# Gate/up products: high and low activations side by side in one 512-wide matmul

## The chip, the cores and the metric

One core of a Trainium2 chip runs the whole kernel in one launch. The metric is device time in microseconds. The kernel before took 2802.89 us, the median of 3 runs (2801.14 to 2803.51).

## The reference, cut to what matters

The program is one layer of a hybrid encoder on 512 tokens of width 2048: an adaLN-conditioned token mixer, a layer norm, then a SwiGLU sublayer of width 5632, all in float32. The change lies in the first half of the SwiGLU:

```python
def swiglu(h, w_gate, w_up, w_down):
    return (jax.nn.silu(h @ w_gate) * (h @ w_up)) @ w_down
...
x = layer_norm(ALPHA * x + (1.0 + gt_m) * y, ln1_g[l], ln1_b[l])
h = x * (1.0 + sc_f) + sh_f
y = swiglu(h, w_gate[l], w_up[l], w_down[l])
```

## The kernel before, in words

**Precision.** Every float32 operand is cut into a rounded high part (ScalarE, a copy to the matmul's type) and the remainder as low part (VectorE, a subtraction): `split`, lines 275 to 277. A product is then three matmuls in `mm3` (lines 239 to 243): high x high, and the two cross terms. For gate/up the weights are stationary (128x128) and the activations are moving.

**Seven products.** Gate and up each multiply 2048 x 512 activations (transposed: `m_hi`, `m_lo`) by 2048 x 5632 weights. This is done as a 2x2 block scheme with seven products in place of eight: weight blocks 11, 12, 21, 22 and their sums S1 to S4, against quarters of the activations and their block sums R4, R6, R7 (R5 goes into the m tiles). A quarter has 256 tokens, so each moving operand is 256 columns wide. The order in a group is `SEVEN = ("p1", "q7", "r6", "p2", "q5", "q4", "p3")` (line 127). p1, p2, q5 and p3 read the m tiles, q7, r6 and q4 the block sums, whose tiles hold high and low side by side. V (p1, r6, q5, p3), Y (q7, q4) and A (p2) are three PSUM banks per group (`CHAIN`); V is read between its products.

**Groups and order.** There are 44 groups `("gu", n)`: n // 2 is the pair of column blocks, n % 2 is gate or up. A gate and the up behind it make a pair: the up's results are multiplied into the gate's Silu. The first four groups (`NPRE`) run in another order, beside the end of the first layer norm; the other 40 run their seven products one behind the other. All is written out by hand and each engine works in program order. The main loop (lines 1601 to 1638) does for each product `step`:

- `prepare(step + 3)`: the high part (ScalarE, `whi`) and low part (VectorE, `wlo`) of the weights three products ahead, 4 buffer pairs in turn;
- `gu_product`: 8 k-steps of `mm3`, 24 matmuls;
- `gu_use`: what follows the product: ScalarE copies or Silu, VectorE adds, subtractions and multiplies, straight from PSUM;
- `add_behind`: VectorE sums of weight blocks: S3 and S1 three steps ahead of a group, S2 two ahead, S4 two steps into it (1024 wide, lines 1284 to 1293).

At the end of an up group `give` forms four more sums and sends seven results by POOL's queue to DRAM for the down projection. `fetch_behind` loads weight blocks on SP's queue four to eight steps ahead. POOL is held to the pace by a one-element copy of ScalarE's eviction at q7 and q5 (line 1627). The down projection (512-wide matmuls) follows.

**Lines to follow.** 277 and 276 (low and high part), 1086 to 1109 (m tiles are filled), 1141 to 1218 (layer norm and block sums into m and R tiles), 1354 to 1432 (`factor`, `gu_product`, `gu_use`).

Of the kernel before, what the change touches and what calls it, by code (L numbers as in the profile page):

```python
# [25 lines left out]
FT = mybir.dt.float32  # L26
# [5 lines left out]
P = 128  # L32
D = 2048
T = 512
# [106 lines left out]
def layer_kernel(ctx, tc, ws, wa, wada, xt, x, cin, bada, lbl, ghg, gcq, gckv, ln1c, lnrow, ident, lvm, dist, out):  # L141
# [17 lines left out]
    def big(name, dt=FR):  # L159
        return bp.tile([P, 4, T], dt, name=name, tag="big")  # L160
# [936 lines left out]
        W.held["out", 3, i] = hold_out  # L1097


    m_hi, m_lo = [], []  # L1100
    for j in range(KD):
        if j % 4 == 0:
            m_hi.append(big(f"mhi{j // 4}"))
            m_lo.append(big(f"mlo{j // 4}"))
# [4 lines left out]
        split(sa, m_hi[j // 4][:, j % 4], m_lo[j // 4][:, j % 4])  # L1109
# [31 lines left out]
    def finish1(t):  # L1141


        mv1[t] = mv = ln_scale(st1[t], "mv1")
        s = slice(t * P, t * P + P)
        z = zt.pop(t)
        for c in (2, 3, 0, 1):
            if t == NT - 1 and c < 2:
                nc.scalar.activation(z[:, c], z[:, c], AF.Identity, scale=mv[:, 3:4], bias=mv[:, 4:5])
            else:  # L1150
                nc.vector.tensor_scalar(z[:, c], z[:, c], mv[:, 0:1], mv[:, 3:4], op0=OP.subtract, op1=OP.mult)
        raws = first_raws() if t == 0 else None
        if t == NT - 1:
            second.append(passing("h22"))
        for _ in range(1 if t < NT - 1 else 3):
            yield
        for pair in (2, 0):
            bs = []
            for c in (pair, pair + 1):
                ps = bank("zt")  # L1160
                for k in range(4):
                    nc.tensor.transpose(ps[:, k * P:k * P + P], z[:, c, k * P:k * P + P], id_t)
                bs.append((c, ps))
            for c, ps in bs:
                h2 = hraw[t, c] = raws[c] if raws else second[0][:, c - 2] if second and c >= 2 else heap("h2")
                for k in range(4):
                    n = 4 * c + k
                    a, b = h2[:, k * P:k * P + P], ps[:, k * P:k * P + P]
                    nc.scalar.activation(a, b, AF.Identity, scale=colA[:, n:n + 1], bias=colB[:, n:n + 1])
                if t < 2 or c >= 2:  # L1170
                    v = h2.rearrange("p (k q) -> p k q", k=4)
                    nc.vector.tensor_copy(m_hi[c][:, :, s], v)
                    nc.vector.tensor_sub(m_lo[c][:, :, s], v, m_hi[c][:, :, s].bitcast(FT))
            yield

    sums = {}

    def put(v, hi, lo):

        v = v.rearrange("p (k q) -> p k q", k=4)  # L1180
        nc.scalar.activation(hi, v, AF.Copy)
        nc.vector.tensor_sub(lo, v, hi.bitcast(FT))

    def block_sums():


        for i in ("R7", "R6", "R5", "R4"):
            raw = {}
            for t in (0, 1):
                for c in range(2):  # L1190
                    h11, h12, h21, h22 = (hraw.get(at) for at in ((t, c), (t + 2, c), (t, c + 2), (t + 2, c + 2)))
                    if i == "R7":
                        raw[t, c] = h22
                        nc.vector.tensor_sub(h22, h12, h22)
# [12 lines left out]
            if i == "R4":  # L1207
                second.clear()
            if i != "R5":
                sums[i] = [passing(f"{i}_{c}", FR) for c in range(2)]  # L1210
            for t, c in list(raw):
                s = slice(t * P, t * P + P)
                s2 = slice(t * P + 2 * P, t * P + 3 * P)
                if i == "R5":
                    put(raw.pop((t, c)), m_hi[c][:, :, s2], m_lo[c][:, :, s2])
                else:
                    put(raw.pop((t, c)), sums[i][c][:, :, s], sums[i][c][:, :, s2])
                yield

    def mh(k):  # L1220
        return m_hi[k // 4][:, k % 4], m_lo[k // 4][:, k % 4]

    def piece(w, n):

# [128 lines left out]

    def factor(i, k):

        if i[0] == "p":
            c, cols = k // 4 + 2 * (i != "p1"), slice(0, 2 * P) if i != "p3" else slice(2 * P, T)
        elif i == "q5":
            c, cols = k // 4, slice(2 * P, T)
        else:  # L1360
            s = sums["R" + i[1]][k // 4][:, k % 4]
            return s[:, :2 * P], s[:, 2 * P:]
        return m_hi[c][:, k % 4, cols], m_lo[c][:, k % 4, cols]

# [22 lines left out]

    def gu_use(u):
        n, i = u.group[1], u.i
        p, up = n // 2, n % 2  # L1390
        ps = acc[n, CHAIN[i]][:, :H]
        t = tmp.setdefault(n, {})
        if i == "p1":
            t["e"] = heap("e")
            nc.scalar.activation(t["e"][:, :H], ps, AF.Copy)
        elif i == "q7":
            t["yv"] = heap("yv")
            nc.scalar.activation(t["yv"][:, :H], ps, AF.Copy)
            acc_copy[:] = [t["yv"][:, :1]]
        elif i == "r6":  # L1400
            nc.scalar.activation(t["yv"][:, H:], ps, AF.Copy)
        elif i == "p2":
            e = t.pop("e")[:, :H]
            if up:
                nc.vector.tensor_add(e, e, ps)
                nc.vector.tensor_mul(act[p][:, :H], act[p][:, :H], e)
            else:
                a = act[p] = heap("act")
                nc.vector.tensor_add(a[:, :H], e, ps)
                nc.scalar.activation(a[:, :H], a[:, :H], AF.Silu)  # L1410
        elif i == "q5":
            vq = heap("vq")[:, :H]
            t["c"] = heap("c") if up else heap("act")
            nc.scalar.activation(vq, ps, AF.Copy)
            acc_copy[:] = [vq[:, :1]]
            nc.vector.tensor_sub(t["c"][:, H:], t["yv"][:, :H], vq)
        elif i == "q4":
            c = t.pop("c")
            nc.vector.tensor_sub(c[:, :H], ps, t.pop("yv")[:, H:])
            if up:  # L1420
                nc.vector.tensor_mul(act[p + NP2], act[p + NP2], c)
            else:
                act[p + NP2] = c
                nc.scalar.activation(c, c, AF.Silu)
# [176 lines left out]
    for step in range(len(steps)):  # L1601
# [25 lines left out]
            nc.gpsimd.tensor_copy(pace, acc_copy[0])  # L1627
            more(1)
        if step == nsteps - 1:
            del m_hi, m_lo  # L1630
            mh = None
# [129 lines left out]
```

## Time and profile before

| | |
|---|---|
| median of 3 runs | 2802.89 us |
| profiled execution | 2800.09 us, of which span 2798.0 us |
| granted TensorE clock, mean | 0.995 |
| TensorE busy | 2750.3 us (98%), 16090 matmuls |
| VectorE busy | 2040.0 us (73%) |
| ScalarE busy | 1158.3 us (41%) |
| POOL busy | 675.6 us (24%) |

The profile is one execution. Times of rows are us from the span's start; durations of groups are ns. A row of the timeline gives start, duration, engine, line, operation, output <- inputs, shape, count, and in brackets the idle time of its engine before it with what ended that. PE is TensorE, DVE VectorE, ACT ScalarE. Matmuls are pipelined: their durations overlap, and their pace is read from starts.

### The profile page before, as it was taken

How to read it: one execution, taken by the hardware profiler on the slowest of the kernel's cores; microseconds unless marked ns; L12 is line 12 of the kernel's file. 1: busy time of each engine (PE TensorE's matmuls, PEld its weight loads, DVE VectorE, ACT ScalarE, POOL GpSimd, SP SyncE). 2: the span in 40 equal slices, each digit the busy share in tenths (PEclk: the TensorE clock that was granted, in tenths of full speed). 3: DMA queues.
4: the chain of work that ended last, by engine and by line, in shares of the span. 5: the costliest groups of instructions: out<-in, count | busy, mean ns of one | idle time of the engine just before them, and what ended most of it. 6: DMA issues, size and time to landing. Idle time of an engine off the chain costs nothing.

```text
span 2798.0 us, 41846 instructions
## 1 busy us (share of the span) xinstructions
PE 2750.3 (98%) x16090; PEld 2421.6 (87%) x16090; DVE 2040.0 (73%) x2892; ACT 1158.3 (41%) x1724; POOL 675.6 (24%) x911
## 2 busy tenths in 40 slices
PE   8999999999999999999999999999999998999997
PEld 6878888888888888788889999999999998887886
DVE  7877687778862678545767777777777776776697
ACT  4334434242322556222236444444444444554453
POOL 0011132433010575421210212221222213443000
PEclk9999999999999999999999999999999999999999
DMA  9866545555984896996945556665556677888774
GB/s 381 310 212 207 167 159 176 173 178 187 320 287 144 231 283 209 271 282 188 282 156 174 182 188 178 190 183 179 197 177 194 174 189 229 274 277 276 242 257 157
DMA packets 179273, 609.85 MB, mean 218 GB/s; under 512 B 23201, under 2 KB 23505, under 8 KB 176001
## 3 DMA queue, kind: packets, MB, share of 16 engines
q1 hardware_dynamic: 126866, 430.18, 44.8%
q0 software_dynamic: 51776, 176.44, 23.5%
q8 instruction: 126, 2.06, 0.3%
q14 instruction: 73, 0.60, 0.1%
q10 hardware_dynamic: 432, 0.57, 0.1%
HBM read 564.09 MB, written 149.70 MB: 255 GB/s over the span
## 4 chain that ended last, share of the span: by engine, by line
PE 90%; DVE 4%; DMA 3%; issue 2%; ACT 1%; POOL 1%; SPq 0%; DVEq 0%; POOLq 0%; ACTq 0%
PE gb L233 6%; PE y L233 6%; PE ga L233 6%; PE V L243 6%; PE V L241 6%; PE V L242 6%; PE qb L233 3%; PE pb L233 3%; PE g L233 3%; PE v L233 3%; PE Y L241 3%; PE Y L243 3%; PE Y L242 3%; PE pa L233 3%; PE early L233 2%; PE dnV L242 2%
## 5 line engine op out<-in xcount | busy, mean ns | idle before, releaser
L277 DVE TENSOR_TENSOR wlo<-raw,whi 128x1024 fp32r<-128x1024 f32 x376 | 468.4, 1253 | 235.4 <-ACT whi L276 235.3
L276 ACT ACTIVATE whi<-raw 128x1024 fp32r<-128x1024 f32 x376 | 397.5, 1058 | 345.2 <-PE dnV L243 132.8
L363 DVE TENSOR_TENSOR wlo<-raw,whi 128x1024 fp32r<-128x1024 f32 (+1 forms) x228 | 284.3, 1250 | 112.3 <-ACT whi L351 111.9
L351 ACT ACTIVATE whi<-raw 128x1024 fp32r<-128x1024 f32 (+1 forms) x228 | 233.7, 1038 | 194.8 <-DVE raw L1086 72.3
L243 PE MATMUL V<-mhi,wlo 128*128 128x256 f32 x1056 | 298.7, 283 | 0.0
L241 PE MATMUL V<-mhi,whi 128*128 128x256 f32 x1056 | 298.6, 283 | 0.0
L242 PE MATMUL V<-mlo,whi 128*128 128x256 f32 x1056 | 298.4, 283 | 0.0
L242 PEld LDWEIGHTS V<-mlo,whi 128*128 128x128 f32 x1056 | 202.2, 191 | 0.0
L241 PEld LDWEIGHTS V<-mhi,whi 128*128 128x128 f32 x1056 | 202.2, 191 | 0.0
L243 PEld LDWEIGHTS V<-mhi,wlo 128*128 128x128 f32 x1056 | 202.2, 191 | 0.0
L241 PE MATMUL Y<-R,whi 128*128 128x256 f32 x704 | 196.1, 279 | 2.2 <-ACT whi L276 2.2
L243 PE MATMUL Y<-R,wlo 128*128 128x256 f32 x704 | 195.6, 278 | 1.8 <-DVE wlo L277 1.8
L242 PE MATMUL Y<-R,whi 128*128 128x256 f32 x704 | 195.7, 278 | 0.0
L242 PE MATMUL dnV<-wlo,fhi 128*128 128x512 f32 x352 | 139.1, 395 | 10.4 <-DVE wlo L277 10.4
L243 PE MATMUL dnV<-whi,flo 128*128 128x512 f32 x352 | 138.7, 394 | 0.0
L241 PE MATMUL dnV<-whi,fhi 128*128 128x512 f32 x352 | 137.9, 392 | 0.2 <-DVE V L1495 0.2
L241 PEld LDWEIGHTS Y<-R,whi 128*128 128x128 f32 x704 | 133.3, 189 | 2.4 <-ACT whi L276 2.4
L243 PEld LDWEIGHTS Y<-R,wlo 128*128 128x128 f32 x704 | 133.0, 189 | 2.2 <-DVE wlo L277 2.2
L242 PEld LDWEIGHTS Y<-R,whi 128*128 128x128 f32 x704 | 133.2, 189 | 0.0
L276 ACT ACTIVATE whi<-wrow 128x1024 fp32r<-128x1024 f32 x80 | 84.4, 1055 | 84.7 <-DVE wrow L1284 84.7
L997 POOL DMA_DIRECT2D sum_dn<-in_ws x132 | 97.1, 816 | 57.9 <-DMA sum_dn<-in_ws 49.6
L233 PE MATMUL ga<-hThi,whi 128*128 128x512 f32 x256 | 102.0, 398 | 0.0
(453 smaller groups left out, 7740.0 us busy)
## 6 DMA issues: line engine op xcount, KB each, us to landing
raw<-in_ws SPq DMA_DIRECT2D x414, 512.0 KB, 5.0
sum_dn<-in_ws POOLq DMA_DIRECT2D x132, 512.0 KB, 8.6
raw<-in_wada SPq DMA_DIRECT2D x128, 512.0 KB, 5.2
raw<-sum_dn SPq DMA_DIRECT2D x88, 512.0 KB, 4.8
rawb<-in_wada SPq DMA_DIRECT2D x22, 1024.0 KB, 12.0
sum_dn<-sum_dn POOLq DMA_DIRECT2D x44, 512.0 KB, 4.9
wrow<-in_ws SPq DMA_DIRECT2D x40, 512.0 KB, 6.6
sum_gu<-in_ws POOLq DMA_DIRECT2D x24, 512.0 KB, 9.4
```

What stands on the lines that cost most here:

```text
L233: mmul(*a, **k)
L241: f(ps, ahi, bhi, start=first, stop=False, **k)
L242: f(ps, ahi, blo, start=False, stop=False, **k)
L243: f(ps, alo, bhi, start=False, stop=last, **k)
L276: nc.scalar.activation(hi, src, AF.Copy)
L277: engine.tensor_sub(lo, src, hi.bitcast(FT))
L351: nc.scalar.activation(hi, src, AF.Copy)
L363: nc.vector.tensor_sub(lo, src, hi.bitcast(FT))
L997: nc.gpsimd.dma_start(d_sum[g, dst], block(g, src), **({"accum_op": OP.add} if add else {}))
```

## The change

The high and low parts of the activations lie side by side in one tile, so that one matmul with the high weights streams both (512 columns, a whole bank: high x high in its left half, high x low in its right). The low weights are multiplied by the high part alone, 256 columns, accumulated into the right half. Two matmuls and two weight loads per k-step take the place of three. The two halves are added behind PSUM, by VectorE, in `gu_use`. The m tiles hold two k blocks each with high and low in turn, and the operations that fill them from the layer norm and for R5 are cut in two. The first four groups add the halves of q7, r6 at once, into half a tile, the others keep 512-wide intermediates.

```diff
-    m_hi, m_lo = [], []
+    m_t = []
+    def mh(k):
+        return m_t[k // 2][:, 2 * (k % 2)], m_t[k // 2][:, 2 * (k % 2) + 1]
+    def mparts(c, s):
+        for n in range(2):
+            v = m_t[2 * c + n].rearrange("p (k h) q -> p k h q", h=2)
+            yield slice(2 * n, 2 * n + 2), v[:, :, 0, s], v[:, :, 1, s]
...
-                    nc.vector.tensor_copy(m_hi[c][:, :, s], v)
-                    nc.vector.tensor_sub(m_lo[c][:, :, s], v, m_hi[c][:, :, s].bitcast(FT))
+                    for k, hi, lo in mparts(c, s):
+                        nc.vector.tensor_copy(hi, v[:, k])
+                        nc.vector.tensor_sub(lo, v[:, k], hi.bitcast(FT))
...
     def factor(i, k):
+        if i[0] == "p" or i == "q5":
+            k += 8 * (i in ("p2", "p3"))
+            cols = slice(0, 2 * P) if i in ("p1", "p2") else slice(2 * P, T)
+            v = m_t[k // 2][:, 2 * (k % 2):2 * (k % 2) + 2, cols]
+            return v, v[:, 0]
+        s = sums["R" + i[1]][k // 4][:, k % 4].rearrange("p (h q) -> p h q", h=2)
+        return s, s[:, 0]
...
-        ps = acc[n, name][:, :H]
+        ps = acc[n, name]
+        wide = ps.rearrange("p (h q) -> p h q", h=2)
         for k in range(8):
             w = slice(k * P, k * P + P)
-            mm3(ps, whi[:, w], wlo[:, w], *factor(i, k), i in FRESH and k == 0, k == 7, f=mmul, skip_group_check=True)
+            both, hi = factor(i, k)
+            mmul(wide, whi[:, w], both, start=i in FRESH and k == 0, stop=k == 7, skip_group_check=True)
+            mmul(wide[:, 1], wlo[:, w], hi, start=False, stop=k == 7, skip_group_check=True)
...
+        M, X = ps[:, :H], ps[:, H:]
+        copy, add, sub = nc.scalar.activation, nc.vector.tensor_add, nc.vector.tensor_sub
+        def whole(v, name):
+            if n < NPRE:
+                if "yv" not in t:
+                    t["yv"] = heap("yv")
+                h = t["yv"][:, :H] if name == "y" else t["yv"][:, H:]
+                copy(h, M, AF.Copy)
+                add(h, h, X)
+            else:
+                h = heap(name)
+                copy(h, ps, AF.Copy)
+            t[name] = h
+            acc_copy[:] = [h[:, :1]]
         if i == "p1":
-            nc.scalar.activation(t["e"][:, :H], ps, AF.Copy)
+            copy(t["e"], ps, AF.Copy)
         elif i == "p2":
-            e = t.pop("e")[:, :H]
+            e = t.pop("e")
+            add(e, e, ps)
             if up:
-                nc.vector.tensor_add(e, e, ps)
-                nc.vector.tensor_mul(act[p][:, :H], act[p][:, :H], e)
+                add(e[:, :H], e[:, :H], e[:, H:])
+                nc.vector.tensor_mul(act[p][:, :H], act[p][:, :H], e[:, :H])
             else:
-                nc.vector.tensor_add(a[:, :H], e, ps)
-                nc.scalar.activation(a[:, :H], a[:, :H], AF.Silu)
+                add(a[:, :H], e[:, :H], e[:, H:])
+                copy(a[:, :H], a[:, :H], AF.Silu)
         elif i == "q5":
-            nc.vector.tensor_sub(t["c"][:, H:], t["yv"][:, :H], vq)
+            copy(vq, ps, AF.Copy)
+            if n < NPRE:
+                sub(c[:, H:], y, vq[:, :H])
+                sub(c[:, H:], c[:, H:], vq[:, H:])
+            else:
+                sub(y, y, vq)
+                add(c[:, H:], y[:, :H], y[:, H:])
         elif i == "q4":
-            nc.vector.tensor_sub(c[:, :H], ps, t.pop("yv")[:, H:])
+            if n < NPRE:
+                sub(c[:, :H], M, v)
+                add(c[:, :H], c[:, :H], X)
+            else:
+                sub(v, ps, v)
+                add(c[:, :H], v[:, :H], v[:, H:])
         elif up:
-            nc.vector.tensor_mul(a[:, H:], a[:, H:], ps)
+            z = heap("z")[:, :H]
+            copy(z, M, AF.Copy)
+            add(z, z, X)
+            nc.vector.tensor_mul(a[:, H:], a[:, H:], z)
         else:
-            nc.scalar.activation(act[p][:, H:], ps, AF.Silu)
+            z = act[p][:, H:]
+            copy(z, M, AF.Copy)
+            add(z, z, X)
+            copy(z, z, AF.Silu)
```

## Rows read from the trace of the kernel before

**Rows 1.** Page, part 1: busy us (share of the span) and instructions of each engine.
```profile
PE 2750.3 (98%) x16090; PEld 2421.6 (87%) x16090; DVE 2040.0 (73%) x2892; ACT 1158.3 (41%) x1724; POOL 675.6 (24%) x911
```
**Rows 2.** Windows: stretch, length, busy (count) of PE, PEld, DVE, ACT, POOL; clock; DMA.
```profile
1474.00:1550.00 76.00, 70.64 (x580) 69.38 (x580) 58.57 (x82) 47.75 (x81) 4.27 (x8) 0.98 0.56 180
1506.00:1509.00 3.00, 3.00 (x16) 3.00 (x16) 2.97 (x6) 0.68 (x2) 0.00 (x0) 0.50 0.53 175
1921.31:1960.67 39.36, 39.36 (x339) 39.36 (x338) 31.05 (x37) 18.12 (x25) 8.07 (x16) 1.00 0.55 186
```
**Rows 3.** Timeline of VectorE: a gate group, then two rows of the up group.
```profile
1921.31 1.22 DVE L1293 TENSOR_TENSOR raw<-raw,wrow 128x1024 f32<-128x1024 f32 x1
1923.71 1.23 DVE L277 TENSOR_TENSOR wlo<-raw,whi 128x1024 fp32r<-128x1024 f32 x1 [1.19 <-ACT whi L276]
1924.85 0.41 DVE L1409 TENSOR_TENSOR act<-e,A 128x256 f32<-128x256 f32 x1
1926.70 1.22 DVE L277 TENSOR_TENSOR wlo<-raw,whi 128x1024 fp32r<-128x1024 f32 x1 [1.43 <-ACT whi L276]
1927.85 0.42 DVE L1416 TENSOR_TENSOR act<-yv,vq 128x256 f32<-128x256 f32 x1
1928.18 1.22 DVE L1284 TENSOR_TENSOR wrow<-raw 128x1024 f32<-128x1024 f32 x1
...
1934.48 1.23 DVE L277 TENSOR_TENSOR wlo<-raw,whi 128x1024 fp32r<-128x1024 f32 x1 [1.21 <-ACT whi L276]
1935.70 1.23 DVE L277 TENSOR_TENSOR wlo<-wrow,whi 128x1024 fp32r<-128x1024 f32 x1
1936.92 1.22 DVE L277 TENSOR_TENSOR wlo<-raw,whi 128x1024 fp32r<-128x1024 f32 x1
1939.13 1.22 DVE L277 TENSOR_TENSOR wlo<-raw,whi 128x1024 fp32r<-128x1024 f32 x1 [0.98 <-ACT whi L276]
1940.27 1.22 DVE L1293 TENSOR_TENSOR raw<-raw,wrow 128x1024 f32<-128x1024 f32 x1
...
1946.70 0.43 DVE L1416 TENSOR_TENSOR c<-yv,vq 128x256 f32<-128x256 f32 x1 [0.88 <-ACT vq L1414]
...
1960.67 1.22 DVE L1293 TENSOR_TENSOR raw<-raw,wrow 128x1024 f32<-128x1024 f32 x1
```
**Rows 4.** Timeline of TensorE: first matmuls of p1, q7, r6 and p2.
```profile
1912.26 0.28 PE L241 MATMUL V<-mhi,whi 128*128 128x256 f32 x1
...
1915.14 0.29 PE L241 MATMUL Y<-R,whi 128*128 128x256 f32 x1
...
1917.88 0.28 PE L241 MATMUL V<-R,whi 128*128 128x256 f32 x1
...
1920.60 0.28 PE L241 MATMUL A<-mhi,whi 128*128 128x256 f32 x1
```
**Rows 5.** Timeline of TensorE in the output projection, 512 wide; 24 matmuls lie between.
```profile
1370.30 0.39 PE L233 MATMUL y<-whi,mlo 128*128 128x512 f32 x1
...
1375.74 0.39 PE L233 MATMUL y<-whi,mlo 128*128 128x512 f32 x1
```
**Rows 6.** Single lines: durations in ns (minimum, median, maximum), first and last start, form.
```profile
L1405 DVE TENSOR_TENSOR e<-e,A x22: 410/414/416, 1489.7 to 2338.1; 128x256 f32<-128x256 f32 x22
L1503 DVE TENSOR_TENSOR E<-E,dnA x4: 676/679/683, 2720.7 to 2725.0; 128x512 f32<-128x512 f32 x4
L1491 ACT ACTIVATE E<-dnV x4: 577/592/597, 2411.7 to 2415.7; 128x512 f32<-128x512 f32 x4
```
**Rows 7.** Timeline of ScalarE at the end of the gate group.
```profile
1934.36 0.36 ACT L1430 ACTIVATE act<-V 128x256 f32<-128x256 f32 x1
1934.62 1.05 ACT L276 ACTIVATE whi<-wrow 128x1024 fp32r<-128x1024 f32 x1
1935.57 0.37 ACT L1395 ACTIVATE e<-V 128x256 f32<-128x256 f32 x1
...
1937.76 0.38 ACT L1398 ACTIVATE yv<-Y 128x256 f32<-128x256 f32 x1 [0.87 <-PE Y L243]
```

More of the change, by code (lines that the diff above doesn't have):

```diff
@@ L1097, in layer_kernel @@
         W.held["out", 3, i] = hold_out
-    m_hi, m_lo = [], []
+    m_t = []
[5 more added lines that the diff above has]
+            yield slice(2 * n, 2 * n + 2), v[:, :, 0, s], v[:, :, 1, s]
     for j in range(KD):
-        if j % 4 == 0:
-            m_hi.append(big(f"mhi{j // 4}"))
-            m_lo.append(big(f"mlo{j // 4}"))
+        if j % 2 == 0:
+            m_t.append(big(f"m{j // 2}"))
         more(2)
@@ L1108, in layer_kernel @@
         nc.vector.tensor_add(sa, sa, sb)
-        split(sa, m_hi[j // 4][:, j % 4], m_lo[j // 4][:, j % 4])
+        split(sa, *mh(j))
         if j + AHEAD < KD:
@@ L1171, in finish1, with put @@
                     v = h2.rearrange("p (k q) -> p k q", k=4)
-                    nc.vector.tensor_copy(m_hi[c][:, :, s], v)
-                    nc.vector.tensor_sub(m_lo[c][:, :, s], v, m_hi[c][:, :, s].bitcast(FT))
+                    for k, hi, lo in mparts(c, s):
+                        nc.vector.tensor_copy(hi, v[:, k])
+                        nc.vector.tensor_sub(lo, v[:, k], hi.bitcast(FT))
             yield
     sums = {}
-    def put(v, hi, lo):
+    def put(v, parts):
         v = v.rearrange("p (k q) -> p k q", k=4)
-        nc.scalar.activation(hi, v, AF.Copy)
-        nc.vector.tensor_sub(lo, v, hi.bitcast(FT))
+        parts = list(parts)
+        for k, hi, lo in parts:
+            nc.scalar.activation(hi, v[:, k], AF.Copy)
+        for k, hi, lo in parts:
+            nc.vector.tensor_sub(lo, v[:, k], hi.bitcast(FT))
     def block_sums():
@@ L1214, in block_sums @@
                 if i == "R5":
-                    put(raw.pop((t, c)), m_hi[c][:, :, s2], m_lo[c][:, :, s2])
+                    put(raw.pop((t, c)), mparts(c, s2))
                 else:
-                    put(raw.pop((t, c)), sums[i][c][:, :, s], sums[i][c][:, :, s2])
+                    put(raw.pop((t, c)), [(slice(0, 4), sums[i][c][:, :, s], sums[i][c][:, :, s2])])
                 yield
-    def mh(k):
-        return m_hi[k // 4][:, k % 4], m_lo[k // 4][:, k % 4]
     def piece(w, n):
@@ L1354, in factor @@
     def factor(i, k):
[L1356 to L1363, printed above, removed]
+        if i[0] == "p" or i == "q5":
[5 more added lines that the diff above has]
+        return s, s[:, 0]
     H = 2 * P
@@ L1390, in gu_use @@
         p, up = n // 2, n % 2
-        ps = acc[n, CHAIN[i]][:, :H]
+        ps = acc[n, CHAIN[i]]
+        M, X = ps[:, :H], ps[:, H:]
+        copy, add, sub = nc.scalar.activation, nc.vector.tensor_add, nc.vector.tensor_sub
         t = tmp.setdefault(n, {})
+        def whole(v, name):
[10 more added lines that the diff above has]
+            acc_copy[:] = [h[:, :1]]
@@ L1393, in gu_use @@
         if i == "p1":
             t["e"] = heap("e")
-            nc.scalar.activation(t["e"][:, :H], ps, AF.Copy)
+            copy(t["e"], ps, AF.Copy)
         elif i == "q7":
-            t["yv"] = heap("yv")
-            nc.scalar.activation(t["yv"][:, :H], ps, AF.Copy)
-            acc_copy[:] = [t["yv"][:, :1]]
+            whole(ps, "y")
         elif i == "r6":
-            nc.scalar.activation(t["yv"][:, H:], ps, AF.Copy)
+            whole(ps, "v")
         elif i == "p2":
-            e = t.pop("e")[:, :H]
+            e = t.pop("e")
@@ L1411, in gu_use @@
         elif i == "q5":
-            vq = heap("vq")[:, :H]
-            t["c"] = heap("c") if up else heap("act")
-            nc.scalar.activation(vq, ps, AF.Copy)
+            vq = heap("vq")
+            c = t["c"] = heap("c") if up else heap("act")
+            copy(vq, ps, AF.Copy)
             acc_copy[:] = [vq[:, :1]]
-            nc.vector.tensor_sub(t["c"][:, H:], t["yv"][:, :H], vq)
-        elif i == "q4":
-            c = t.pop("c")
-            nc.vector.tensor_sub(c[:, :H], ps, t.pop("yv")[:, H:])
+            y = t.pop("y")
@@ new lines, in gu_use @@
+            if n < NPRE:
[4 more added lines that the diff above has]
+                add(c[:, H:], y[:, :H], y[:, H:])
+        elif i == "q4":
+            c, v = t.pop("c"), t.pop("v")
+            if n < NPRE:
+                sub(c[:, :H], M, v)
+                add(c[:, :H], c[:, :H], X)
+                del t["yv"]
+            else:
+                sub(v, ps, v)
+                add(c[:, :H], v[:, :H], v[:, H:])
@@ L1423, in gu_use @@
                 act[p + NP2] = c
-                nc.scalar.activation(c, c, AF.Silu)
+                copy(c, c, AF.Silu)
         elif up:
             a, b = act.pop(p), act.pop(p + NP2)
-            nc.vector.tensor_mul(a[:, H:], a[:, H:], ps)
+            z = heap("z")[:, :H]
+            copy(z, M, AF.Copy)
+            add(z, z, X)
+            nc.vector.tensor_mul(a[:, H:], a[:, H:], z)
             give(p, a, b)
         else:
-            nc.scalar.activation(act[p][:, H:], ps, AF.Silu)
+            z = act[p][:, H:]
+            copy(z, M, AF.Copy)
+            add(z, z, X)
+            copy(z, z, AF.Silu)
         if i in DONE:
@@ L1629, in layer_kernel @@
         if step == nsteps - 1:
-            del m_hi, m_lo
-            mh = None
+            m_t = None
             sums.clear()
```

## The prediction

> **What bounds the kernel now.** I read the page's busy shares first: TensorE 98%, VectorE 73% [rows 1]. A share over the whole span hides stages, so next I took one period of the stage that the change touches. Gate/up works through 44 groups of seven products, and groups come in pairs, a gate and an up, which differ in what follows the products. From one S4 sum to the S4 two groups on (1921.31 to 1960.67) the pair takes 39.36 us; TensorE is busy in all of it, VectorE in 31.05 us [rows 2]. There are 20 such pairs, since the first four groups run in another order. So TensorE is the bound, and a first reading would give VectorE 8.3 us of room in a pair.
>
> The third view corrects that reading. VectorE works in program order, and its timeline shows what its idle time waits for [rows 3]. After S4 (1921.31) it stands 1.19 us before the low half of p3's weights, because ScalarE must round the sum that VectorE has only just written. The same happens after S2 (1.21 us before 1934.48), and after p2 of a gate group, where ScalarE does the Silu before it rounds the next weights (1.43 us before 1926.70). These waits are a loop VectorE to ScalarE to VectorE with nothing else in line. The up half repeats the first two. Per pair that is 2 x (1.19 + 1.21) + 1.43 = 6.23 us which no faster TensorE and no later VectorE takes away. Only two waits are for TensorE: 0.98 us (before 1939.13, where ScalarE had first waited for the end of q7 at 1937.76 [rows 7]) and 0.88 us (before 1946.70, for the copy of q5's result). VectorE's true room is therefore 1.86 us in 39.36, and its own chain is 37.5 us per pair.
>
> **TensorE's gain.** Per k-step three 256-wide matmuls become one 512-wide and one 256-wide; the columns stay 768. What can be saved is the cost beside the columns. The p1 product, on m, takes 24 matmuls from 1912.26 to 1915.14, so 120.0 ns each. The r6 product, on block sums, takes 24 from 1917.88 to 1920.60, so 113.3 ns [rows 4]. For 512 columns the output projection shows 24 in 1370.30 to 1375.74, 226.7 ns [rows 5], which is twice 113.3. So on m a k-step goes from 360.0 to 346.7 ns, and on block sums it stays at 340 ns. A group has four products on m and three on sums: 4 x 8 x 13.3 ns = 0.43 us less per group, 0.85 per pair, 17 us over 20 pairs. The trace has no 512-wide matmul whose moving operand is two blocks of 256 with a gap, as m now is. Its price lies between 226.7 ns and 240 (two slow 256-wide ones, no gain); I take 226.7, the one measured at that width. (240 would take the gain away and change nothing below, where TensorE is no longer the bound.) 2464 weight loads go too, but they are already hidden beside matmuls.
>
> The Trainium skill (TensorE: Matmul & The Clock Gate, section Back-to-back issue gap) gives a fixed 2.5 ns per matmul beside its columns. By it the merge would save 2.5 ns in each of 2464 k-steps, an estimate of 6 us, and the first rival below would end near 2797 us, not measurably faster. The trace disagrees: 6.7 to 13.3 ns stand beside the 106.7 that 256 columns take at 2.4 GHz.
>
> **What VectorE gets in return.** The product now fills the whole bank: main part in one half, cross terms in the other, and someone must add the halves. Durations: 256 wide from PSUM 0.414 us, 512 wide 0.679 us; ScalarE's 512-wide copy 0.592 us [rows 6]. A dependent operation starts some 0.03 us after the end of the one before, an independent one after 0.33 us (1927.85 to 1928.18) [rows 3].
> - p2, q5 and q4 each had one 256-wide operation. Each now has a 512-wide one and then a dependent 256-wide add: 0.71 us until the add can start, and the add stands where the old operation stood. That is +0.71 us, three times a group, 4.26 per pair.
> - p3 of an up group was a multiply straight from PSUM. Now ScalarE copies the main half (covered by the weight subtraction, 1.14 us), and an add stands ahead of the multiply: +0.45 us.
> - p3 of a gate group had no VectorE work: Silu came straight from PSUM. Now it is copy, VectorE add, Silu, and ScalarE rounds p2's next weights only behind that Silu. From the subtraction at 1934.48 to the next at 1935.70 it was 1.22 us. Now it is 1.14 (subtraction, pitch 1923.71 to 1924.85) + 0.45 (add) + 0.26 (Silu's pitch) + 1.08 (rounding and handing on) = 2.93 us [rows 7]: +1.71, of which 1.3 is a new wait. A fourth loop has been made, where there was none.
> - Behind it ScalarE is late with the next two: rounding 0.95 us and a copy of 0.26 + 0.22 for its wider form, 1.43 each. Before they took 1.22 and 2.21 (1935.70, 1936.92, 1939.13). That is +0.21, and -0.78, in which the wait for TensorE of 0.98 us is swallowed.
> - p1, q7 and r6 have their copies 0.22 us longer on ScalarE, which is busy 18.12 us of the pair [rows 2]; hidden, save where just counted. The evictions that the next product on the same bank needs have one product of 2.7 us between [rows 4], so the longer copy does not reach TensorE. Loads, SP's and POOL's queues keep their order; a pair that gets longer gives them more time.
>
> **The sum.** Gate group: 1940.27 - 1921.31 = 18.96, + 3 x 0.71 + 1.71 + 0.21 - 0.78 = 22.2 us. Up group: 1960.67 - 1940.27 = 20.40, - 0.88 (its wait for TensorE) + 3 x 0.71 + 0.45 = 22.1 us. The pair is 44.3 us against 38.5 that TensorE then needs: VectorE's chain becomes the bound, and TensorE waits 5.8 us in each pair for low weights. Cross-check from the other side: 31.05 busy + 5.2 added + 6.23 old loop waits + 1.7 new ones (1.3 + 0.2 + 0.2) = 44.2. Against 39.36 that is +4.97 us, times 20 = +99 us.
>
> The first four groups run at 1474 to 1550 beside the layer norm's tail, VectorE 58.6 us busy in 76, TensorE idle 5.4 [rows 2]. They get 4 x 0.71 + 8 x 0.45 + 8 x 0.71 + 4 x 0.45 = 13.9 us more VectorE work, about 1 us more for the copies of m cut in two, and TensorE 1.7 us less. Bounds 0 (all in idle time) and +15; half of it falls where VectorE has no gaps, so I take +4. The down projection does not change. Together 2800.1 (span 2798.0 and 2.1 around it) + 99 + 4 = 2903; the median of the runs lies 2.8 us above the profiled one, so **2906 us**.
>
> **Rivals.**
> - *VectorE swallows it* (faster). If the loop waits could be filled, 31.05 + 5.2 = 36.3 us fit into 38.5 and TensorE stays the bound: -0.85 x 20 - 2 = -19, so 2784 us. For it: the busy share. Against it: every wait in the timeline stands directly behind the sum or activation that causes it, and VectorE takes nothing out of order. It decides by whether the chain stays under 38.5 us; mine lies 5.8 above. Chance 0.11, with the case that only some of the adds cost.
> - *Chain without new waits* (slower, less). If Silu and copies overlap better than I lay them out, only busy time is added: 5.2 - 1.86 = 3.3 us per pair, +66, so 2869 us.
> - *The clock falls in the new gaps* (slower, more). After TensorE's pauses near 1502 and 1505 the granted clock was 0.50 at 1506 to 1509, the 1.2 GHz level [rows 2]. Gaps of 1 to 2.5 us will come in every group. A stretch of 3 us at half speed loses 1.5 us of matmuls; two in a pair, 3 us, fit into the 5.8 us. If two thirds reach the path it is 2 x 20 = +40, with the early bound +11: 2957 us.
> - *No change*: gain and chain cancel; it needs 1.0 us per pair less than TensorE's own room allows. Chance 0.04.
>
> **How the numbers follow.** VectorE-bound in one of its three forms 0.85, own range 2866 to 2957; faster 0.11; no change 0.04. What a measurement can tell from no change is 0.2%, some 6 us. The range 2852 to 2957 leaves out the faster case, no change and a little of the far ends.
>
> **What would show it.** Right: pairs near 44 us, TensorE idle before matmuls of the low weights with VectorE's subtraction as releaser, VectorE about 36 us busy in a pair with no wait left for TensorE, a wait before p2's subtraction in gate groups only. Matmul pitch on m of 226.7 and 120 ns inside a product shows the gain. Wrong: pairs of 38.5 us with TensorE unbroken; or TensorE held by something else, such as ScalarE's evictions or late loads.

## The result, and the profile of the changed kernel

The changed kernel takes 2936.42 us (median; 2931.97 to 2942.69), the kernel before beside it 2802.01 (2799.49 to 2803.51): a ratio of 1.0482, interval 1.0461 to 1.0504. It is slower by 134 us where 104 were forecast. In the profiled executions the span grew from 2798.0 to 2933.5 us, +135.5, and the starts of the stages' first matmuls say where: gate/up starts 2.9 us earlier, its first four groups take 93.28 us instead of 88.98 (+4.3), the 20 pairs 917.96 instead of 787.20 (+130.8), what follows 3.3 more.

The page, parts 1 and 4 (busy time and instructions of each engine; the chain that ended last, by engine; the last line is the chain of the kernel before). It answers to [rows 1]: 2464 matmuls fewer, and still more time busy, with the same 73% on VectorE. The chain, 90% TensorE before, now runs 15% over VectorE and 6% over ScalarE.
```profile
PE 2803.9 (96%) x13626; PEld 2337.6 (80%) x13626; DVE 2153.9 (73%) x3104; ACT 1202.7 (41%) x1772; POOL 686.7 (23%) x911
...
PE 69%; DVE 15%; ACT 6%; issue 6%; DMA 2%; POOL 1%; SPq 0%; ACTq 0%; DVEq 0%; POOLq 0%
```
```profile
PE 90%; DVE 4%; DMA 3%; issue 2%; ACT 1%; POOL 1%; SPq 0%; DVEq 0%; POOLq 0%; ACTq 0%
```
The windows (stretch, length, busy time of PE, PEld, DVE, ACT, POOL, clock, DMA), for [rows 2]: the four early groups, the 20 pairs, then an up group, a gate group and a stretch inside it.
```profile
1466.14:1559.42 93.28, 84.66 (x465) 71.57 (x464) 76.77 (x122) 55.35 (x93) 4.81 (x9) 0.98 0.53 173
1559.42:2477.38 917.96, 839.43 (x4483) 712.84 (x4481) 721.65 (x865) 405.94 (x543) 184.76 (x300) 0.95 0.52 159
1960.25:1983.50 23.25, 23.21 (x131) 19.85 (x130) 19.53 (x27) 10.02 (x13) 5.80 (x10) 1.00 0.59 166
1983.50:2005.85 22.35, 18.50 (x96) 15.57 (x95) 16.55 (x19) 10.16 (x14) 2.90 (x6) 0.89 0.42 152
2002.35:2007.70 5.35, 5.35 (x17) 4.57 (x18) 4.31 (x4) 2.33 (x3) 1.14 (x2) 0.51 0.33 110
```
The pairs now hold TensorE idle for 78.5 of 918 us, and their granted clock is 0.95: for about a tenth of the stage it was at 0.50, the 1.2 GHz level, as in the last row. VectorE idles 196 us in the same stretch, more than TensorE, and yet it is the bound. VectorE's timeline of that gate group, for [rows 3], shows how:
```profile
1983.50 1.22 DVE L1304 TENSOR_TENSOR raw<-raw,wrow 128x1024 f32<-128x1024 f32 x1
1985.90 1.22 DVE L277 TENSOR_TENSOR wlo<-raw,whi 128x1024 fp32r<-128x1024 f32 x1 [1.19 <-ACT whi L276]
1987.04 0.68 DVE L1433 TENSOR_TENSOR e<-e,A 128x512 f32<-128x512 f32 x1
1987.76 0.42 DVE L1439 TENSOR_TENSOR act<-e 128x256 f32<-128x256 f32 x1
1989.62 1.23 DVE L277 TENSOR_TENSOR wlo<-raw,whi 128x1024 fp32r<-128x1024 f32 x1 [1.43 <-ACT whi L276]
...
1998.86 1.23 DVE L277 TENSOR_TENSOR wlo<-raw,whi 128x1024 fp32r<-128x1024 f32 x1 [1.21 <-ACT whi L276]
2000.01 0.41 DVE L1477 TENSOR_TENSOR act<-act,V 128x256 f32<-128x256 f32 x1
2001.85 1.23 DVE L277 TENSOR_TENSOR wlo<-wrow,whi 128x1024 fp32r<-128x1024 f32 x1 [1.43 <-ACT whi L276]
2003.28 1.23 DVE L277 TENSOR_TENSOR wlo<-raw,whi 128x1024 fp32r<-128x1024 f32 x1 [0.20 <-ACT whi L276]
2004.71 1.23 DVE L277 TENSOR_TENSOR wlo<-raw,whi 128x1024 fp32r<-128x1024 f32 x1 [0.20 <-ACT whi L276]
2005.85 1.22 DVE L1304 TENSOR_TENSOR raw<-raw,wrow 128x1024 f32<-128x1024 f32 x1
2009.41 1.23 DVE L277 TENSOR_TENSOR wlo<-raw,whi 128x1024 fp32r<-128x1024 f32 x1 [2.34 <-ACT whi L276]
```
The new 512-wide operations (L1433) and their 256-wide adds (L1439) are there. So is the wait that the forecast drew: 1.43 us at 2001.85, the subtraction for p2's weights behind the Silu of p3. Further down, at 2009.41, stands a wait that was not forecast: 2.34 us where S4's loop costs 1.19. ScalarE's timeline, for [rows 7], leads to it:
```profile
1998.73 0.37 ACT L1476 ACTIVATE act<-V 128x256 f32<-128x256 f32 x1
2000.45 0.42 ACT L1478 ACTIVATE act<-act 128x256 f32<-128x256 f32 x1 [1.35 <-DVE act L1477]
2000.77 1.04 ACT L276 ACTIVATE whi<-wrow 128x1024 fp32r<-128x1024 f32 x1
2001.72 0.58 ACT L1426 ACTIVATE e<-V 128x512 f32<-128x512 f32 x1
2002.20 1.05 ACT L276 ACTIVATE whi<-raw 128x1024 fp32r<-128x1024 f32 x1
...
2007.84 0.60 ACT L1420 ACTIVATE v<-V 128x512 f32<-128x512 f32 x1 [3.16 <-PE V L1398]
2008.33 1.05 ACT L276 ACTIVATE whi<-raw 128x1024 fp32r<-128x1024 f32 x1
```
p1's result is copied at 2001.72, behind a Silu that waited for VectorE and behind a rounding. TensorE accumulates r6 on the same bank and so stood until then, as its own timeline shows (for [rows 4]; first and last matmul of r6, then p2's first):
```profile
2002.35 0.79 PE L1397 MATMUL V<-R,whi 128*128 128x512 f32 x1 [3.60 <-ACT e L1426]
...
2007.42 0.38 PE L1398 MATMUL V<-R,wlo 128*128 128x256 f32 x1
2007.63 0.40 PE L1397 MATMUL A<-m,whi 128*128 128x512 f32 x1
```
After the pause of 3.60 us r6 runs at the 0.50 clock, its matmuls 0.63 and 0.41 us long, and takes 5.28 us instead of 2.8. So ScalarE waits 3.16 us for r6's result (until 2007.84), p3's rounding behind it is late (2008.33), and VectorE waits 2.34 us. This is one of the longer cases. The pause of 3.5 to 3.6 us comes in each of the 20 pairs, ahead of the up group's r6; in 18 of them r6 then took 4.02 to 5.29 us, and in two it took 2.92, at full clock.

TensorE's and VectorE's waits over the 20 pairs (total, times, longest): VectorE's for rounded weights, TensorE's for p1's copy, VectorE's for q5's copy, and that of TensorE's weight loads (PEld) for low weights.
```profile
DVE wlo L277 <- ACT whi L276: 172.1, 160, 2.4
...
PE V L1397 <- ACT e L1426: 71.7, 23, 3.6
...
DVE y L1451 <- ACT vq L1444: 13.4, 18, 0.8
...
PEld A L1398 <- DVE wlo L277: 4.0, 20, 0.2
```

### The profile page after: what moved, and what is told of

It reads as the page before. It is cut to its first block, busy times and chain, and to the rows that moved or that the text cites. A ratio compares the mean times of both kernels' runs of the same rounds, so it can differ in the third digit from the quotient of the medians.

```text
span 2933.5 us, 37274 instructions
## 1 busy us (share of the span) xinstructions
PE 2803.9 (96%) x13626; PEld 2337.6 (80%) x13626; DVE 2153.9 (73%) x3104; ACT 1202.7 (41%) x1772; POOL 686.7 (23%) x911
## 3 DMA queue, kind: packets, MB, share of 16 engines
q8 instruction: 107, 1.75, 0.2%
## 4 chain that ended last, share of the span: by engine, by line
PE 69%; DVE 15%; ACT 6%; issue 6%; DMA 2%; POOL 1%; SPq 0%; ACTq 0%; DVEq 0%; POOLq 0%
PE V L1397 6%; PE gb L233 6%; PE y L233 6%; PE ga L233 6%; DVE wlo L277 5%; ACT whi L276 5%; PE qb L233 3%; PE pb L233 3%; PE V L1398 3%; PE g L233 3%; PE v L233 3%; PE early L233 3%; PE pa L233 2%; PE s L233 2%; PE dnV L242 2%
## 5 line engine op out<-in xcount | busy, mean ns | idle before, releaser
L1397 PE MATMUL V<-m,whi 128*128 128x512 f32 x1056 | 377.4, 399 | 6.3 <-ACT vq L1444 6.3
L1398 PE MATMUL V<-m,wlo 128*128 128x256 f32 x1056 | 296.1, 280 | 0.0
L1397 PE MATMUL Y<-R,whi 128*128 128x512 f32 x704 | 253.1, 398 | 3.3 <-ACT whi L276 3.3
L1397 PEld LDWEIGHTS V<-m,whi 128*128 128x128 f32 x1056 | 198.2, 188 | 59.9 <-ACT vq L1444 12.7
L1397 PE MATMUL V<-R,whi 128*128 128x512 f32 x352 | 160.4, 482 | 72.3 <-ACT e L1426 71.7
L1398 PEld LDWEIGHTS V<-m,wlo 128*128 128x128 f32 x1056 | 199.3, 189 | 0.0
L1397 PEld LDWEIGHTS Y<-R,whi 128*128 128x128 f32 x704 | 133.0, 189 | 35.6 <-ACT whi L276 3.9
L233 PE MATMUL y<-whi,m 128*128 128x512 f32 x448 | 138.7, 390 | 0.0
L1397 PE MATMUL A<-m,whi 128*128 128x512 f32 x352 | 127.8, 399 | 0.0
L277 DVE TENSOR_TENSOR wlo<-wrow,whi 128x1024 fp32r<-128x1024 f32 x80 | 97.9, 1224 | 28.6 <-ACT whi L276 28.6
L1398 PE MATMUL V<-R,wlo 128*128 128x256 f32 x352 | 113.0, 321 | 1.5 <-DVE wlo L277 1.5
```

Of the source, the lines that this page charges most:

```text
L233: mmul(*a, **k)
L277: engine.tensor_sub(lo, src, hi.bitcast(FT))
L1397: mmul(wide, whi[:, w], both, start=i in FRESH and k == 0, stop=k == 7, skip_group_check=True)
L1398: mmul(wide[:, 1], wlo[:, w], hi, start=False, stop=k == 7, skip_group_check=True)
```

## The experiments

Two ends to test: are the additions behind PSUM the cause (theory A), or the wide matmul, its layout, or something else; and what makes 6.5 us per pair of a forecast 4.97. "Ratio" is against the kernel before on the same chip, whose medians were 2801.53 to 2803.14.

**e1, three narrow matmuls, additions kept.**
```diff
-            mmul(wide, whi[:, w], both, start=i in FRESH and k == 0, stop=k == 7, ...)
+            if i in FRESH and k == 0:
+                mmul(wide, whi[:, w], both, start=True, stop=False, ...)
+            else:
+                mmul(wide[:, 0], whi[:, w], hi, start=False, stop=k == 7, ...)
+                mmul(wide[:, 1], whi[:, w], both[:, 1], start=False, stop=False, ...)
```


> The merge alone undone: tiles, full bank and all work behind PSUM as in the changed kernel, but the high weights are multiplied by the high and the low part in two 256-wide matmuls (one k-step in three products of a group stays 512 wide, to open the bank). Theory A (VectorE's chain behind PSUM is the cost): the time stays at that of the changed kernel, 2920 to 2945 us, pairs near 46 us, because TensorE needs only some 39 us per pair either way. Theory B (the wide matmuls, their pace or their clock, are the cost): most of the 134 us comes back, 2800 to 2830 us.

2928.68 us (2923.53 to 2930.93), ratio 1.0434 (1.0418 to 1.0450). Nearly all of the loss is there without the wide matmul. Pairs take 45.45 us on the mean (this and the lengths of pairs below are from the starts of p2's first matmuls, 19 pairs; the change has 45.98 so).

**e2, the wide matmul without the additions.** The changed products and layout, with the old use of each result on one half.
```diff
     def gu_use(u):
-        ps = acc[n, CHAIN[i]]          # and all that the change adds below
+        ps = acc[n, CHAIN[i]][:, :H]   # and the body of the kernel before
```


> The merge kept, the halves not added: what follows the products is that of the kernel before and reads the left half alone, so the cross terms of gate/up are left out of the output. Theory A: VectorE's chain is 37.5 us per pair again, TensorE the bound; its products take 2.81 to 2.83 us each in the changed kernel's trace, 7 x 2.82 = 19.7 us per group against 19.68 before, so 2795 to 2810 us: the merge gains nothing. The prediction's gain on TensorE (0.85 us per pair) would give 2783 us. Theory B: 2900 us or more.

2802.93 us (2797.36 to 2808.12), ratio 0.9994 (0.9985 to 1.0004). So all of the slowdown comes with what was added behind PSUM (adds and wider reads, which no run takes apart), and the merge by itself gains nothing that can be measured. TensorE's timeline of e2 (a k-step of q5, then the first matmul of q4, on block sums, and of p3):
```profile
1924.37 0.40 PE L1397 MATMUL V<-m,whi 128*128 128x512 f32 x1
1924.61 0.28 PE L1398 MATMUL V<-m,wlo 128*128 128x256 f32 x1
1924.73 0.40 PE L1397 MATMUL V<-m,whi 128*128 128x512 f32 x1
...
1927.20 0.39 PE L1397 MATMUL Y<-R,whi 128*128 128x512 f32 x1
...
1930.01 0.39 PE L1397 MATMUL V<-m,whi 128*128 128x512 f32 x1
```
A k-step on m takes 0.35 to 0.36 us, a product 2.81 to 2.83; one on block sums takes 2.81 (q7, q4) or 2.83 (r6). Before they took 2.86 to 2.88 and 2.72 to 2.74 [rows 4]: m won 0.05 us per product, the sums lost 0.07 to 0.11. A group of seven is 19.73 us against 19.68, where 19.25 was forecast.

**e3, the layout alone** (the kernel before, m stored as the change stores it, three narrow matmuls).
```diff
...
+            v = m_t[k // 2][:, 2 * (k % 2):2 * (k % 2) + 2, cols]
+            return v[:, 0], v[:, 1]
...
```


> The kernel before with the m tiles laid out as in the changed one (high and low of a k block in neighbouring rows of one tile), three 256-wide matmuls per k-step and everything behind PSUM as before. Theory A1 (the 120 ns of a 256-wide matmul on m, against 113.3 on block sums, comes from high and low lying in different tiles): 113.3 ns on m too, 4 x 8 x 3 x 6.7 ns = 0.64 us per group, some 28 us less: 2775 us, TensorE still the bound. Theory A2 (it comes from where the tiles lie, or from the gap of 256 columns between high and low): 120 ns stays, 2795 to 2808 us.

2802.37 us (2800.10 to 2808.44), ratio 0.9999 (0.9989 to 1.0008); products on m 2.86 to 2.88 us, as before. The layout and its extra small copies cost nothing that can be measured.

**e4, p3's add and Silu of a gate group two products later.**
```diff
-            add(z, z, X)
-            copy(z, z, AF.Silu)
...
+                later.append(rest)     # the two lines above, run after the next q7's copy
...
+        if i == "q7" and later:
+            later.pop()()
```


> The changed kernel with one loop taken away: in a gate group the add and the Silu behind p3 come two products later, behind q7's copy of the next group, so that ScalarE no longer rounds p2's next weights and copies p1's result behind that Silu. Theory A (the new loop at p3 costs 1.43 us of VectorE waiting and holds TensorE at r6 through the copy of p1's result, and the clock falls in that pause): pairs go from 46 to 43 or 44 us, 2875 to 2900 us. Rival (only the added busy time counts, a wait removed here comes back elsewhere): 2925 to 2940 us.

2904.19 us (2900.00 to 2908.17), ratio 1.0349 (1.0333 to 1.0365): between the two theories. Pairs take 44.24 us. VectorE's timeline shows why it was not more:
```profile
1946.84 0.41 DVE L1480 TENSOR_TENSOR act<-act,V 128x256 f32<-128x256 f32 x1
1948.68 1.23 DVE L277 TENSOR_TENSOR wlo<-raw,whi 128x1024 fp32r<-128x1024 f32 x1 [1.43 <-ACT whi L276]
1949.82 1.22 DVE L1304 TENSOR_TENSOR raw<-raw,wrow 128x1024 f32<-128x1024 f32 x1
```
The 1.43 us had moved to the next weights: the add (L1480) and Silu stand ahead of another rounding now. Moving this link of the loop moved the wait with it. TensorE's longest pause before r6 was halved, and it waited there more often: its waits between 1600 and 2300 us, in the change and in e4 (total, times, longest).
```profile
PE V L1397 <- ACT e L1426: 53.9, 17, 3.6
```
```profile
PE V L1398 <- ACT e L1427: 40.9, 32, 1.8
```
The clock fell in e4 as well, after pauses of 1.75 to 1.85 us: 15 products r6 took 4.0 to 4.5 us. Here that cost nothing, since from an r6 to the one two groups on it took 44.2 us behind slow and fast ones alike (44.5 once). So most of e4's gain is that r6 no longer came too late for VectorE; the loop itself, moved, cost nearly what it had (44.24 us a pair against e7's 44.46 below).

**e5, m as runs of 512 columns** (kernel before, hi and lo of one half of the columns in one run, three narrow matmuls).
```diff
...
+            v = m_t[k // 2][:, 2 * (k % 2) + (i not in ("p1", "p2"))]
+            return v[:, :2 * P], v[:, 2 * P:]
...
```


> The kernel before with the m tiles laid out as the block sums are: for each k block and each half of the tokens 256 high columns and right behind them 256 low ones; three 256-wide matmuls and all else as before. The layout with high and low in neighbouring rows (e3) left a matmul on m at 120 ns. Theory A1' (what makes block sums fast is that high and low are one run of 512 columns): 113.3 ns on m, 0.64 us less per group, 2773 to 2780 us. Theory A2 (it is the place of the tiles or something else): 120 ns, 2798 to 2808 us.

2802.23 us (2798.83 to 2805.86), ratio 1.0002 (0.9993 to 1.0011); products on m still 2.86 to 2.88 us. The order of the columns doesn't set the pitch, the time from one matmul's start to the next.

**e6, the loops opened.** All of the change's work, but S2 issued right behind S1 and S4 a product earlier, so that other work stands between a sum and its rounding, and the three Silus of a gate group one product later.
```diff
-        for ahead, what in ((3, "S3"), (3, "S1"), (2, "S2"), (-2, "S4")):
+        for ahead, what in ((3, "S3"), (3, "S1"), (3, "S2"), (-1, "S4")):
...
+        due, later[:] = later[:], []      # at the head of gu_use
...
-                copy(a[:, :H], a[:, :H], AF.Silu)
+                later.append(lambda: copy(v, v, AF.Silu))   # so for all three
...
+        for do in due:                    # at its end
+            do()
```


> The changed kernel with every operation, but the order changed so that VectorE no longer waits for ScalarE directly behind its own result: S2 is summed right behind S1, S4 one product earlier, and the three Silus of a gate group are issued one product later, behind the next weights. Theory A (the in-order waits, 6.2 us old and 1.4 us new per pair, make the chain too long; busy time alone is 31.05 + 0.2 + 5.2 = 36.5 us per pair): TensorE is the bound again at 7 x 2.82 = 19.7 us per group, 39.5 per pair, 2803 to 2825 us. Rival (the busy time added is what costs, wherever it stands): 2860 us or more.

2807.31 us (2801.60 to 2814.31), ratio 1.0021 (1.0011 to 1.0030). 129 of the 134 us are back with not one operation less. A pair of e6, and VectorE's waits for rounded weights from 1600 to 2300 us in e6 and in the change:
```profile
1921.31:1960.80 39.49, 39.49 (x227) 34.33 (x226) 35.97 (x45) 20.53 (x27) 8.42 (x17) 1.00 0.51 184
```
```profile
DVE wlo L277 <- ACT whi L276: 31.8, 55, 1.0
```
```profile
DVE wlo L277 <- ACT whi L276: 130.1, 121, 2.4
```
VectorE is busy 35.97 of 39.49 us and TensorE in all of them. In the change 36.1 busy microseconds per pair (721.65 / 20) were the bound by their waits; 36.0 with few waits are none. Which of the three reorderings did most is not shown.

**e7, the clock held.** The change, with 12 matmuls that nobody reads, put into TensorE's pause ahead of r6 in up groups.
```diff
+            if i == "r6" and n % 2 and n >= NPRE:
+                warm, r = bank("warm"), sums["R7"][0][:, 0]
+                for _ in range(12):
+                    mmul(warm, r[:, :P], r, start=True, stop=True)
...
```


> The changed kernel with 12 further 512-wide matmuls into a bank of their own ahead of r6 in each up group, in the pause of some 3.6 us in which TensorE waits for the copy of p1's result; they leave the result as it is. Theory A (the clock falls in that pause and r6 at half speed, some 1.5 to 2.5 us longer, lies on the loop through its copy and the rounding of S4): granted clock 1.00 through the stage, 20 pairs x 1.2 to 1.6 us, 2903 to 2915 us. Rival (r6 at half speed fits into TensorE's room): 2930 to 2942 us, the clock up all the same.

2906.07 us (2904.11 to 2906.90), ratio 1.0369 (1.0352 to 1.0386): 30 us less than the change. The 20 pairs, then VectorE's and TensorE's waits in them:
```profile
1560.00:2449.35 889.35, 862.45 (x4725) 729.21 (x4723) 718.00 (x863) 407.77 (x543) 179.84 (x300) 1.00 0.54 164
```
```profile
DVE wlo L277 <- ACT whi L276: 161.7, 160, 1.5
...
PE V L1402 <- ACT e L1431: 20.6, 40, 0.9
```
The clock stays at 1.00, no wait of TensorE is over 0.9 us, r6 takes 2.91 to 2.93 us, and a pair takes 44.46 us. VectorE waits 10 us less for rounded weights than in the change, and not at all for q5's copy. The trace of the change says the same: from one up group's r6 to the next it took 44.45 and 44.44 us behind the two that ran at full clock, and 45.60 to 46.82 behind the others.

**e8, other places for the big tiles** (kernel before, each slot 192 bytes longer, so that m's tiles start at changing places).
```diff
-        return bp.tile([P, 4, T], dt, name=name, tag="big")
+        return bp.tile([P, 4 * T + 48], dt, ..., tag="big")[:, :4 * T].rearrange("p (a b) -> p a b", a=4)
```


> The kernel before with the eight large tiles (the m tiles among them) each 192 bytes longer per partition, so that each begins at another place within 2048 bytes; nothing else differs. It asks what makes a 256-wide matmul 113.3 ns on block sums and 120 ns on m, now that the layout of high and low is ruled out (e3, e5). Theory P (where a tile begins in its partition decides): the pitch on m differs from tile to tile between 113 and 120 ns, time 2775 to 2805 us. Rival Q (it is not the place: the tile's neighbours, its contents or the work beside it): 120 ns in all of them, 2798 to 2808 us.

2808.44 us (2802.96 to 2810.93), ratio 1.0019 (1.0010 to 1.0029). Products on m fell to 2.83 to 2.84 us, the pitch by tile lay between 112 and 124 ns; those on block sums, whose tiles did not move, kept 2.72. But the 512-wide matmuls on moved tiles rose, in the output projection from some 227 ns to 230 to 232, which cost more: in the profiled executions gate/up took 7.2 us less and what lies ahead of it 10.3 more.

**e9, e10, e11: the place put to use.** e9 is e6 with the layout of e5; e10 adds 960 bytes ahead of the block sums and scratch tiles; e11 is the kernel before with those 960 bytes alone.
```diff
+    ctx.enter_context(tc.tile_pool(name="pad", bufs=1, side="right")).tile([P, 240], FT, name="pad")
```


> The version with the loops opened (same work as the change, three reorderings), and m laid out so that the hi and lo halves which a product takes are one run of 512 columns. With the loops open TensorE is the bound (39.45 us per pair), so its pitch should now show in the time. Theory (the pitch follows the place of the moving tile against the weights' tile within 2 KB, and one run of columns is no dearer than the output projection's): the wide matmul on m goes from 233 to about 227 ns, a k-step from 350 to 344, 4 x 8 x 6 ns = 0.19 us per group, 44 groups -8 us: about 2799 us. Rival (the price hangs on the width alone, or VectorE's chain is the bound by then): 2805 to 2812 us, no change from the loops opened.

> The same, and 960 bytes left free at the start of the side that holds the block sums and the scratch tiles, so that their tiles lie at the same phase within 1 KB as the weights. No instruction is added or taken out. Theory (place decides the pitch): the wide matmul on block sums goes from 235 to about 227 ns, and its k-step from 353 to 344; 3 x 8 x 9 ns = 0.22 us per group, -9 us over 44 groups beside the -8 of the layout; the 512-wide matmuls of the projections that read tiles of that side go from 235 to 227 too, some 1150 of them, -8 us: 2775 to 2792 us, provided that VectorE's chain (36 us busy in a pair, few waits left) keeps under 38.7 us. Rival 1 (place plays no part for the wide ones): as the run without the 960 bytes. Rival 2 (VectorE's chain becomes the bound once TensorE is faster): pairs stay near 39.2 us, and only the projections' 8 us come: 2790 to 2800.

> The kernel before with the 960 bytes alone. Theory (place decides the pitch, with opposite sign for the two widths): the 256-wide matmuls on block sums go from 113 to 120 ns, 3 x 24 x 6.7 ns = 0.48 us per group, +21 us over 44 groups; the projections' 512-wide matmuls on that side go from 235 to 227, some 1150 x 8 ns = -9 us: 2810 to 2818 us. Rival (place plays no part): 2802, no change.

e9: 2807.09 us (2805.13 to 2810.18), ratio 1.0015 (1.0005 to 1.0024); e10: 2798.34 (2795.93 to 2803.72), 0.9985 (0.9976 to 0.9994); e11: 2812.41 (2809.45 to 2814.88), 1.0033 (1.0021 to 1.0045). e11 hits its theory, and in its parts: gate/up takes 20.7 us more, what lies ahead of it and behind it 8.2 less. Its products on block sums now take 2.88 us too:
```profile
1903.18 0.28 PE L242 MATMUL V<-R,whi 128*128 128x256 f32 x1
1903.30 0.28 PE L243 MATMUL V<-R,whi 128*128 128x256 f32 x1
...
1906.06 0.28 PE L242 MATMUL A<-mhi,whi 128*128 128x256 f32 x1
```
e9 misses its theory and ends as its rival says; e10 misses its theory too and gets only the projections' part: its gate/up starts 6.1 us earlier than e9's and what follows is 3.7 us shorter, while gate/up itself is 2.4 us longer, with products of 2.82 to 2.83 us (e9: 2.81 to 2.83). When widths alternated, a k-step cost 351 to 354 ns on the mean of a product at both places.

**e12, wide first.** e10 with eight 512-wide matmuls and then eight 256-wide ones in each product.
```diff
         for k in range(8):
...
-            mmul(wide, whi[:, w], both, ...)
-            mmul(wide[:, 1], wlo[:, w], hi, ...)
...
+            mmul(wide, whi[:, w], factor(i, k)[0], ...)
...
+        for k in range(8):
...
+            mmul(wide[:, 1], wlo[:, w], factor(i, k)[1], ...)
```


> The version with the loops opened, the layout and the 960 bytes, and in each product first the eight 512-wide matmuls and then the eight 256-wide ones, instead of one of each in turn. Theory (turning from one width and weight tile to the other costs TensorE some 4 to 7 ns at each k-step, since 512 after 512 took 227 ns and 256 after 256 took 113 or 120 in uniform runs, and the pair in turn 353): a product of 8 x 227 + 8 x 113 or 120 = 2.72 to 2.78 us instead of 2.826; 7 x 0.05 to 0.10 us per group over 44 groups, -15 to -31 us: 2767 to 2783 us if VectorE's chain keeps under 38.9 us in a pair. The low weights are also wanted 1.7 us later in each product, which takes from the wait for them and adds nothing to VectorE's work. Rival 1 (the price of the mixed k-step is in the columns and loads themselves): 2794 to 2802, as without this edit. Rival 2 (VectorE's chain becomes the bound): 2785 to 2798, with TensorE waiting for low weights.

2786.30 us (2785.60 to 2791.84), ratio 0.9948 (0.9934 to 0.9961): 15 us less than the kernel before and 150 less than the change, the fastest version here. It lies 3 us over the theory's range, at the low end of rival 2's; TensorE's timeline speaks for the theory with a smaller size (eight wide, eight narrow, the next product):
```profile
1911.08 2.00 PE L1400 MATMUL A<-m,whi 128*128 128x512 f32 x8
1912.92 1.12 PE L1405 MATMUL A<-m,wlo 128*128 128x256 f32 x8
1913.87 2.00 PE L1400 MATMUL V<-m,whi 128*128 128x512 f32 x8
```
8 x 230 and 8 x 119 ns, so 2.79 us a product and 19.55 a group, without a break. VectorE did not take over: pairs take 39.11 us, and TensorE is busy in all 743.03 us of 19 of them.

## Why the forecast held, and where it fell short

- **Direction and cause** were right, and the bound in the main. Without the additions nothing is lost (e2), with them and without the wide matmul nearly all is (e1). That it is the waits and not the work was the point of the reading of [rows 3]; e6 shows it, since the same operations in another order cost 5 us and not 134. The bound was VectorE's chain with TensorE's r6 as one more link of it, which the main line did not have.
- **VectorE's chain: +4.97 us per pair forecast, +5.10 measured** where the clock stays up (e7, 44.46 against 39.36). In the change the gate group of the rows came to 22.35 us (22.2 forecast), the up group to 23.25 (22.1), and e7's up group, from S4 at 1993.98 to S4 at 2016.07, to 22.09. From p3's subtraction to p2's it took 2.99 us (2.93) with a wait of 1.43 (1.3), and the next two came 1.43 us apart each, as forecast (2003.28, 2004.71).
- **The step that failed** is "the longer copy does not reach TensorE". The copy's length was weighed, and its place was not. It stands behind the Silu and the rounding that the change had just made late: ScalarE's rows from 2000.45 to 2002.20 follow one another in the order of the program, and p1's copy starts at 2001.72, when TensorE has stood for 3.0 us (3.60 us before 2002.35). The forecast had this lateness in VectorE's sum and did not carry it over to TensorE. TensorE was to idle 5.8 us per pair, waiting for low weights; for these it waited 0.2 us a pair (4.0 us in 20 waits), and it got one pause before r6, 71.7 us in 23 waits over the pairs. The Trainium skill (PSUM — Partial Sum Buffer, section Engine vs sequencer instructions) says that the queues of ScalarE and VectorE are strict first in, first out. These rows agree with it.
- **The clock** was therefore a term of the main line, not a rival to it. Behind 18 of the 20 pauses of 3.5 to 3.6 us r6 ran in part or in whole at the 0.50 level, and r6, late by the pause and by the clock, stands in VectorE's loop through ScalarE's copy. TensorE, late by then, also had VectorE wait for q5's copy (13.4 us in 18 waits, none in e7). Held at 1.00 (e7), the 20 pairs take 889.35 us instead of 917.96: 28.6 us, where the rival had priced 40. In spans the forecast was 2901 us and the result 2933.5. Of the 32.5 between them 28.6 is the clock, 3.2 the rest of the pairs, 0.3 the early groups and 3.3 what follows gate/up, less 2.9 ahead of it. That the rival's size was nearly right is partly luck: it took the gaps to be 1 to 2.5 us, twice a pair.
- **Its own signs** came out mixed. VectorE's 36.1 busy us per pair and the wait before p2's subtraction in gate groups came as foretold. TensorE's idle time in front of low weights did not, VectorE still waited for TensorE, and a sign of being wrong came true: TensorE held by one of ScalarE's evictions.
- **TensorE's gain: -0.43 us per group forecast, +0.05 measured** (e2). It failed in two places. 512 columns took 227 ns among their like [rows 5]; next to 256-wide ones a k-step on m came to 352 to 354 ns, not 346.7. On block sums, costed at no change, a k-step went from 340 or 342 ns to 351 or 353. With a third fewer matmuls the products took as long. In the change this didn't show, as TensorE was not the bound; without the additions it would have been an error of 19 us (the first rival's 2784 against the 2803 of e2). The Trainium skill (TensorE: Matmul & The Clock Gate, section Back-to-back issue gap) gives 2.5 ns beside the columns, for an isolated matmul; by that the merge would gain 6 us, an estimate. e2 doesn't bear it out: 6 us less is a ratio of 0.998, below its interval.
- **The early groups**: +4 forecast, +4.3 measured, with luck. The forecast had 14.9 us of added work and let half of it count, which is 7.5; how it came to 4 is not said. The 3.3 us behind gate/up were not forecast. e1, e6 and e7 have 3.0 to 3.4 there too, e2 1.5; their cause stays open.
- **"VectorE swallows it"** failed for the reason given, waits in program order; e6 shows that VectorE would have swallowed the additions (pairs of 39.5) with the order changed too. The gain on TensorE that this rival counted on (pairs of 38.5) was not there.

## What to carry to other kernels

Count an in-order engine's waits together with its work: here an engine at 73% was the bound, and the room that counted was what was left when the waits that follow from its own order were added. Ask of each copy out of PSUM not only how long it is but what stands ahead of it in its queue, and who is stopped by it; here a single pause of 3.6 us cost TensorE its clock as well, in 18 of 20 pairs. Before a matmul is merged for its fixed cost, look for a row with the same mix of widths in the same order.

## What the runs showed of the hardware

- The pitch of a matmul depended on where its moving tile lay. e11 moved the tiles of one side by 960 bytes and nothing else: 256 columns on block sums went from 113 to 120 ns, while 512 columns in the projections that read that side (`pb`) went from 233 to 227. With the 192-byte shifts of e8, 256 columns on m, 120 before, took 112 to 124. Whether the place by itself counts or its distance from the weights' tile, which no run moved for these products, is not shown; what in the chip does this was not found.
- A 512-wide and a 256-wide matmul in turn took 351 to 354 ns on the mean of a product at every place tried with TensorE unbroken (e2, e6, e9, e10); eight and then eight took 349 for the two (e12).
- TensorE's clock fell to the 0.50 level behind 18 of 20 pauses of 3.5 to 3.6 us in the change, and behind 15 pauses of 1.75 to 1.85 us in e4. With 12 unread matmuls in the pause (e7) it stayed at 1.00.
